# A decoder layer on one core: constants on GpSimd's queue, h's steps behind the eviction, background sums moved between stages

## The chip, the cores and the metric

The kernel runs on 1 core of one Trainium2 chip. The core has TensorE (PE in the profile; PEld is its weight load), VectorE (DVE), ScalarE (ACT), GpSimd (POOL) and SyncE (SP); SP and GpSimd also issue DMAs from queues of their own, and each engine runs its instructions in the order of its own queue. The metric is the device time of one execution in microseconds; lower is better. Three runs of the kernel before took 1571.95, 1572.47 and 1573.18 us, median 1572.47.

## The reference

One layer of a decoder trunk in float32, with 256 tokens (T) and a model width of 2048 (D). Cut to what matters here:

```python
mod = jax.nn.silu(c) @ w_ada[l] + b_ada[l]
shift1, scale1, gate1, shift2, scale2, gate2 = jnp.split(mod[:, None, :], N_MOD, axis=-1)
h = rms_norm(x, norm1_gain[l]) * (1 + scale1) + shift1
x = x + gate1 * mixing_sublayer(h, w_in[l], ...)
h = rms_norm(x, norm2_gain[l]) * (1 + scale2) + shift2
x = x + gate2 * swiglu(h, w_ffn_in[l], w_ffn_out[l])

# mixing_sublayer
proj = h @ w_in
(q_sb, k_sb, v_sb, q_dil, k_dil, v_dil, q_gla, k_gla, v_gla, r_gla, a_gla, gate_cols) = jnp.split(proj, idx, axis=-1)
qb = rms_norm(split_heads(q_dil, DIL_HEADS), dil_q_gain)
kb = rms_norm(split_heads(k_dil, DIL_HEADS), dil_k_gain)
o_dil = merge_heads(dilated_mixture(qb, kb, split_heads(v_dil, DIL_HEADS), alibi_slopes(DIL_HEADS)))
g = jax.nn.sigmoid(gate_cols.reshape(b, t, N_BRANCH, d))
y = g[:, :, 0] * (o_sb @ w_br_sb) + g[:, :, 1] * (o_dil @ w_br_dil) + g[:, :, 2] * (o_gla @ w_br_gla)
return y @ w_out
```

The conditioning vector c gives six rows of 2048 numbers (adaLN): shift, scale and gate for the mixer and for the FFN. The mixer has three branches (stick-breaking attention, dilated windows, gated linear attention, GLA), each behind a sigmoid gate.

## The kernel before

**Products.** Every float32 product is done as three products of a shorter kind: a tile of weights (raw, 128 x 1024, two k-rows of 512 columns, 512 KB) is cast to its high part on ScalarE (whi, L179 or L255), the rest is subtracted on VectorE (wlo, L180 or L241, "the split" below), and TensorE takes high x high (L187), high x low (L188) and low x high (L189). A chunk of weights is two k-rows for two token tiles: twelve matmuls of 512 columns. load_weights issues the loads on SP's queue, ahead of use, into raw buffers that come free when cast and split have read them.

**Stages, by time of the profile.** Up to about 205 us the activations h of the mixer are made chunk by chunk, as the columns of shift1 and scale1 come in, and the blocks of w_in are visited over part of k each (visit: seed a PSUM bank with the partial result, L650; products; evict it, L643). One chunk of h is two steps on ScalarE (make_h: L606 for the high part, L610 for the whole) and a subtraction on VectorE (L611). Then the constants of the attention branches are loaded (L926 to L934: k_low, k_bias, k_lvl, w_gla_a, k_dist). To about 400 the rest of the projection, stick-breaking and GLA run. Then comes the norm of the dilated rows (qk_norm: squares L955 on ScalarE, a chain of small instructions L413 to L421, multiplies L963 on VectorE), while TensorE computes blocks 13 and 14 of w_in; among those are the transposes of the normed rows (qk_turn, L975). From 440 gate blocks are computed, from 486 to 590 three gate pairs by a product with fewer multiplications (gate_pair, fast_products, whose sums and differences are VectorE's L221, L241, L292 and L335 to L338), then the branches' y blocks to 660, gate block 3 with the last y block to about 755, w_out to about 860, and the FFN to the end.

**Background work.** The other four rows of adaLN are computed in the background of these stages. A step (ada_segment_steps) loads half a column block of w_ada, 512 KB (L433, on GpSimd's queue), into a buffer of a ring (tags such as AR0, AR1, OD, KC, KD) and sums an earlier one on VectorE against silu(c) (column_mac, L440, "a sum" below, 1.28 us). The function tick paces them: each chunk of weights adds state["rate"], and a step is done when the total reaches one. So a rate of 0.7 is seven steps in ten chunks. A sum is ordered behind the instruction in state["split"], as a rule the last split. L448 and spread (L370 to L393) turn a finished segment's columns into what its users read.

**What sets the order.** The program text and priorities do, through a scheduler that fills each engine's queue; tc.issue_after(x) keeps an instruction behind x in that order, and prio() raises a load or a cast ahead. A queue is then strict: an instruction that waits holds all behind it on its engine.

The rates of the kernel before are:

```python
RATE_IN, RATE_MID, RATE_GATES, RATE_PAIRS, RATE_Y, RATE_LAST = 0.7, 0.7, 0.65, (0.3, 0.12, 0.12), 0.65, 0.68
RATES_OP, RATES_FFN = (0.4, 0.3, 0.0), (0.75, 0.9, 0.7, 0.6)
RATE_FIRST, RATE_NEXT = 0.95, 0.9
```

Of the kernel before, what the change touches and what calls it, by code (L numbers as in the profile page):

```python
# [13 lines left out]
AF = mybir.ActivationFunctionType  # L14
ALU = mybir.AluOpType
# [15 lines left out]
N_DIL = 6  # L31
N_GLA = 4
SEG_SHIFT1, SEG_SCALE1, SEG_GATE1, SEG_SHIFT2, SEG_SCALE2, SEG_GATE2 = range(6)
RATE_IN, RATE_MID, RATE_GATES, RATE_PAIRS, RATE_Y, RATE_LAST = 0.7, 0.7, 0.65, (0.3, 0.12, 0.12), 0.65, 0.68

RATES_OP, RATES_FFN = (0.4, 0.3, 0.0), (0.75, 0.9, 0.7, 0.6)
LOOK = 3
DEFER = 4
AHEAD = 4000
WARM = (8, 2, 2, 2, 1, 2, 2, 4)  # L40
BADA = 58
RATE_FIRST, RATE_NEXT = 0.95, 0.9
BLOCKS_X, BLOCKS_Y, BLOCKS_Z = (1, 2, 3, 4), (5, 6, 7, 8), (9, 10, 11, 12, 0)
TWO = 3
VISITS = ((BLOCKS_Z, 1, 5, 5, 7), (BLOCKS_Y, 3, 7, 7, 9), (BLOCKS_X, 4, 9, 9, 11),
# [15 lines left out]
RANK = 16  # L61
# [25 lines left out]
def trunk(ctx: ExitStack, tc: tile.TileContext, I, out):  # L87
# [69 lines left out]
    def load_weights(src, k0, k1, b, spare=(), ahead=True, late=None):  # L157

        parts = []
        step, w = 2, NB
        with prio() if ahead else nullcontext():
            for ka in range(k0, k1, step):
                n = min(step, k1 - ka)
                raw = raw_tile(state.get("load_raws", ()))
                state["load"] = nc.sync.dma_start(raw[:, :n, :], src[b, :, ka : ka + n, :])
                i = len(spare) - (k1 - ka)
                if i >= 0:  # L170
                    hi = S(spare[i], [P, step, w], F32R)
                    lo = S(spare[i + 1], [P, step, w], F32R)
                else:
                    hi = wp.tile([P, step, w], F32R, tag="whi", name=nm("whi"), bufs=4)
                    lo = wp.tile([P, step, w], F32R, tag="wlo", name=nm("wlo"), bufs=4)
                if i >= 0 and late is not None:
                    state["casts_after"] = late
                with tc.issue_after(state["casts_after"]) if "casts_after" in state else nullcontext():
                    state["cast"] = nc.scalar.copy(hi[:, :n, :], raw[:, :n, :])  # L179
                state["split"] = nc.vector.tensor_tensor(lo[:, :n, :], raw[:, :n, :], hi[:, :n, :].bitcast(F32), op=ALU.subtract)  # L180
                parts += [(hi[:, i, :], lo[:, i, :]) for i in range(n)]
        if late is not None:
            state.pop("casts_after", None)
        return parts
# [294 lines left out]
            if seg == SEG_SCALE1:  # L479
                scaled_gain(mod1[seg], ROW_N1, k, k + 1)  # L480

    def h_due():
        if "h_due" in state:
            make_h(state.pop("h_due"), after=state["cast"])

    def ada_chunks(k0, k1):

# [111 lines left out]
    def make_h(k, early=False, after=None):  # L599

        sh, sc = gains(k)
        src = xT[k // 4][:, k % 4, :]
        hf = scr([P, T])
        hi = hT[0][k // 4][:, k % 4, :]
        with tc.issue_after(after.ins if hasattr(after, "ins") else after) if after is not None else nullcontext():
            nc.scalar.activation(hi, src, AF.Identity, bias=sh, scale=sc)  # L606
        if early:
            nc.vector.tensor_scalar(hf, src, sc, sh, op0=ALU.mult, op1=ALU.add)
        else:
            nc.scalar.activation(hf, src, AF.Identity, bias=sh, scale=sc)  # L610
        nc.vector.tensor_tensor(hT[1][k // 4][:, k % 4, :], hf, hi.bitcast(F32), op=ALU.subtract)  # L611

    def h_at(k, t):
# [9 lines left out]
    def proj_block(k0, k1, b, w=None, carry=False, steps=None, bank=acc_bank):  # L623
        go_on = bool(carried)
        pss = carried.pop() if go_on else [bank([P, NB]) for _ in range(NT)]
        seeded = A[b] is not None and not go_on
        if seeded:

            with prio():
                for t in range(NT):  # L630
                    nc.scalar.copy(pss[t], A[b][:, t, :])
        block(pss, h_at, w_in, k0, k1, b, w=w, go_on=go_on or seeded, more=carry, seeded=seeded or go_on, steps=steps)
        if carry:
            carried.append(pss)
            return
        evict(b, pss)

    def evict(b, pss):
        with prio():
            if A[b] is None:  # L640
                A[b] = S(f"A{b}", [P, NT, NB])
            for t in range(NT):
                nc.scalar.copy(A[b][:, t, :], pss[t])  # L643

    pending = []

# [5 lines left out]
    def visit(k0, k1, b, bank, carry):  # L652
        pss = [bank([P, NB]) for _ in range(NT)]
        seed(b, pss)
        w = load_weights(w_in, k0, k1, b)
        with tc.issue_after(state["cast"].ins):
            for _ in range(min(2, len(pending))):
                evict(*pending.pop(0))
        h_due()
        block(pss, h_at, w_in, k0, k1, b, w=w, go_on=True, more=carry, seeded=True)  # L660
        (carried if carry else pending).append(pss if carry else (b, pss))

# [260 lines left out]
    lvl_f = S("T4", [P, len(GLA_LEVELS) + 1, P])  # L923
    wga = kc[: 2 * RANK, 4:8, :].rearrange("p a b -> p (a b)")
    with prio():
        nc.sync.dma_start(low, I["k_low"])  # L926
        nc.sync.dma_start(bias, I["k_bias"])
        nc.sync.dma_start(lvl_f, I["k_lvl"])
        for i in range(2):
            nc.sync.dma_start(wga[i * RANK : (i + 1) * RANK, :], I["w_gla_a"])  # L930
    nc.scalar.copy(low_r, low)
    nc.gpsimd.tensor_copy(lvl, lvl_f)
    nc.sync.dma_start(near, I["k_dist"][:, 0:2, :])
    nc.sync.dma_start(far, I["k_dist"][:, 2, :])  # L934

    def head(c, t):
        return A[c // 4][:, t, (c % 4) * P : (c % 4 + 1) * P]
# [7 lines left out]
    def qk_norm(parts):  # L945

        n = sum(h1 - h0 for _, h0, h1, _ in parts)
        ss = small([P, NT, n])
        places, o = [], 0
        for b, h0, h1, _ in parts:  # L950
            for t in range(NT):
                for h in range(h0, h1):
                    junk = scr([P, P])
                    i = o + h - h0
                    nc.scalar.activation(junk, heads(b)[:, t, h, :], AF.Square, accum_out=ss[:, t, i : i + 1])  # L955
            places.append(slice(o, o + h1 - h0))
            o += h1 - h0
        r = rsqrt(ss.rearrange("p t h -> p (t h)"), 1.0 / P, [P, NT * n])
        r = r.rearrange("p (t h) -> p t h", t=NT)
        for (b, h0, h1, _), c in zip(parts, places):  # L960
            for t in range(NT):
                v = heads(b)[:, t, h0:h1, :]
                state["split"] = nc.vector.tensor_tensor(  # L963
                    v, v, r[:, t, c].unsqueeze(2).to_broadcast([P, h1 - h0, P]), op=ALU.mult
                )

# [329 lines left out]
        state[name] = quarters  # L1296

    def background():
        for seg in (SEG_SHIFT2, SEG_SCALE2, SEG_GATE1, SEG_GATE2):
            v = gate2_v if seg == SEG_GATE2 else columns_of(f"mod_{seg}")  # L1300
            done = {SEG_GATE1: lambda: rows_of("gate1", v, ("T4", "T5")), SEG_GATE2: lambda: None}.get(seg, lambda: columns(seg, v))
            yield from ada_segment_steps(v, seg, done())
        yield from last_macs()
# [16 lines left out]
    qk_turn(sb_parts[:2], state["mm"].ins)  # L1320
    sb_hi, sb_lo, sb_step = stick_breaking()
    og, og_norms = gla()
    state["rate"] = RATE_NEXT
    for b in range(6, 9):
        proj_block(*LAST[b], b)
    qk_norm(dil_parts)

# [48 lines left out]
    def sums_of_h(p0, n, scratch, tags):  # L1376
        j, c = p0 // 2, slice(0, 2 * n)
        full = S(scratch[0], [P, 4, T])[:, c]
        with tc.issue_after(state["split"].ins):
            nc.vector.tensor_tensor(full, hT[0][j][:, c].bitcast(F32), hT[1][j][:, c].bitcast(F32), op=ALU.add)  # L1380
        sf = S(scratch[1], [P, 4, 2, P])[:, :, :n]
        sums_of(sf, [full[:, :, t * P : (t + 1) * P] for t in range(NT)], slice(0, 2 * n, 2), slice(1, 2 * n, 2))
        if n == 2:
            hi, lo = (S(tag, [P, 4, n, P], F32R) for tag in tags)
        else:
            hl = S(tags[0], [P, 2, 4, n, P], F32R)
            hi, lo = hl[:, 0], hl[:, 1]
        nc.scalar.copy(hi, sf)
        state["split"] = nc.vector.tensor_tensor(lo, sf, hi.bitcast(F32), op=ALU.subtract)
        for m in range(n):  # L1390
            h_sums[p0 + m] = [(hi[:, i, m, :], lo[:, i, m, :]) for i in range(4)]
# [10 lines left out]
    del state["turns"]  # L1402
    gate_block(0, 1, turns)
    sums_of_h(6, 1, ("X1", "X2"), ("T3",))
    gate_block(0, 2)


# [84 lines left out]
    state["raws"] = -1  # L1492
    gate_pair(0, GATE_PAIRS_2, acc_bank, misc_bank, (("X1", "X2"), ("A9", "A10")), ("T0",))
    gate_pair(1, GATE_PAIRS_3, misc_bank, acc_bank, (("A9", "A10"), ("X1", "T0"), ("T4", "T5")), ("X2", "A8"))
    gate_pair(2, GATE_PAIRS_3, acc_bank, misc_bank, (("A9", "A10"), ("T4", "T5")), ("T0", "X2"))
    ring["tags"] = ("AR0", "AR1", "KC", "KD")
    ring["spare"] = 2
# [335 lines left out]
```

## Time and profile before

| | |
|---|---|
| median of 3 runs | 1572.47 us |
| profiled execution, its own time | 1574.92 us |
| its span | 1573.2 us |
| mean granted clock of TensorE | 0.995 |
| ScalarE busy | 919.4 us (58%) |
| GpSimd busy | 72.1 us (5%) |
| data moved | 399.21 MB, mean 254 GB/s |

A page of the profile lists busy times, waits, groups of instructions and DMAs. In a row of waits stand the engine and line that waited, what it waited for, the total, the number and the longest. In a timeline a row is start, duration, engine, line, operation, output and input tiles, and in brackets the idle time before it with what ended it. In a row of windows stand the stretch, its length, then busy time and instructions of PE, PEld, DVE, ACT and POOL, then the granted clock of TensorE (1.00 is full), the mean busy share of the DMA engines, and GB/s. The span is the time from the first to the last instruction; the execution's own time has a little more around it, 1.7 us here.

### The profile page before, as it was taken

The page shows a single profiled execution, that of the slowest core. Times are in us where ns is not written, and L with a number is a line of the kernel's source. Part 1 is how long each engine was busy: PE and PEld are TensorE (multiplying, and loading weights), DVE is VectorE, ACT ScalarE, POOL GpSimd, SP SyncE. Part 2 cuts the span into 40 slices and gives each one's busy share as a digit, 9 for nine tenths or more (in the row PEclk, how much of TensorE's full clock was granted, in tenths as well). Part 3 has the DMA queues.
Part 4 walks back from the last instruction along what each step waited for, and adds up shares of the span by engine and source line. Part 5 has one row for each costly group of instructions (what it writes and reads, how often), then busy time and mean ns, then how long its engine had stood idle before and what let it go on. Part 6 is the DMA issues. An engine that isn't in the chain of part 4 may idle for free.

```text
span 1573.2 us, 20109 instructions
## 1 busy us (share of the span) xinstructions
PE 1549.8 (99%) x7055; PEld 1279.9 (81%) x7055; DVE 1371.3 (87%) x1838; ACT 919.4 (58%) x1294; POOL 72.1 (5%) x139
## 2 busy tenths in 40 slices
PE   9999999999899999999999999999999999999998
PEld 7788878888687878888888888788888888888887
DVE  7898967888788989987977888999999999789886
ACT  7887776865575555444445645556555555455553
POOL 0000010101100000111100000000000000000000
PEclk9999999999899999999999999999999999999999
DMA  9999897767587767999986686665666567656664
GB/s 371 399 388 352 305 365 272 232 205 235 198 305 244 240 233 227 339 330 329 390 279 214 227 293 206 196 205 194 203 203 203 175 200 247 191 190 196 220 212 136
DMA packets 113749, 399.21 MB, mean 254 GB/s; under 512 B 12496, under 2 KB 13392, under 8 KB 113648
## 3 DMA queue, kind: packets, MB, share of 16 engines
q1 hardware_dynamic: 94640, 328.72, 60.7%
q0 software_dynamic: 19008, 69.21, 13.0%
q8 instruction: 55, 0.90, 0.2%
q14 instruction: 46, 0.38, 0.1%
HBM read 393.69 MB, written 4.19 MB: 253 GB/s over the span
## 4 chain that ended last, share of the span: by engine, by line
PE 74%; DVE 13%; issue 5%; DMA 5%; ACT 3%; POOL 0%; DVEq 0%; ACTq 0%; POOLq 0%; SPq 0%
PE acc L188 17%; PE acc L189 17%; PE acc L187 17%; PE misc L188 6%; PE misc L189 6%; PE misc L187 6%; DVE wlo L241 3%; DMA raw<-w_in 2%; DVE A L241 1%; DMA X<-w_in 1%; DVE T L241 1%; DVE OD L241 1%; DVE KD L241 1%; DMA OS<-ada_t 1%; PE misc L1128 1%
## 5 line engine op out<-in xcount | busy, mean ns | idle before, releaser
L188 PE MATMUL acc<-wlo,H 128*128 128x512 f32 (+1 forms) x856 | 335.4, 392 | 4.2 <-DVE wlo L241 2.8
L187 PE MATMUL acc<-whi,H 128*128 128x512 f32 (+1 forms) x856 | 334.9, 393 | 1.9 <-ACT acc L650 1.1
L189 PE MATMUL acc<-whi,H 128*128 128x512 f32 (+1 forms) x856 | 335.3, 392 | 0.1
L179 ACT CAST whi<-raw 128x1024 fp32r<-128x1024 f32 (+1 forms) x172 | 177.4, 1037 | 149.6 <-PE acc L189 90.9
L180 DVE TENSOR_TENSOR wlo<-raw,whi 128x1024 fp32r<-128x1024 f32 (+1 forms) x172 | 205.4, 1201 | 48.5 <-ACT whi L179 46.9
L188 PEld LDWEIGHTS acc<-wlo,H 128*128 128x128 f32 x856 | 161.6, 189 | 38.8 <-DVE wlo L241 3.8
L187 PEld LDWEIGHTS acc<-whi,H 128*128 128x128 f32 x856 | 161.4, 189 | 35.8 <-ACT acc L650 1.5
L189 PEld LDWEIGHTS acc<-whi,H 128*128 128x128 f32 x856 | 161.5, 189 | 33.6 <-DVE H L1571 0.5
L255 ACT CAST whi<-raw 128x1024 fp32r<-128x1024 f32 (+1 forms) x129 | 124.2, 975 | 75.8 <-PE acc L189 32.1
L241 DVE TENSOR_TENSOR wlo<-raw,whi 128x1024 fp32r<-128x1024 f32 (+1 forms) x129 | 143.3, 1124 | 17.4 <-ACT whi L255 16.1
L189 PE MATMUL misc<-whi,H 128*128 128x512 f32 x285 | 110.5, 388 | 0.0
L188 PE MATMUL misc<-wlo,H 128*128 128x512 f32 x285 | 110.4, 388 | 0.0
L187 PE MATMUL misc<-whi,H 128*128 128x512 f32 x285 | 109.4, 388 | 0.0
L189 PE MATMUL acc<-whi,A 128*128 128x512 f32 x221 | 86.0, 389 | 0.0
L187 PE MATMUL acc<-whi,A 128*128 128x512 f32 x210 | 82.1, 391 | 0.0
L188 PE MATMUL acc<-wlo,A 128*128 128x512 f32 x210 | 81.7, 389 | 0.0
L179 ACT CAST whi<-X 128x1024 fp32r<-128x1024 f32 (+1 forms) x49 | 48.7, 999 | 41.0 <-PE acc L189 31.9
L180 DVE TENSOR_TENSOR wlo<-X,whi 128x1024 fp32r<-128x1024 f32 (+1 forms) x49 | 56.4, 1155 | 15.4 <-ACT whi L179 15.3
L188 PEld LDWEIGHTS misc<-wlo,H 128*128 128x128 f32 x285 | 53.5, 188 | 11.0
L189 PEld LDWEIGHTS misc<-whi,H 128*128 128x128 f32 x285 | 53.5, 188 | 11.0
L187 PEld LDWEIGHTS misc<-whi,H 128*128 128x128 f32 x285 | 53.5, 188 | 10.9
L241 DVE TENSOR_TENSOR A<-raw,A 128x1024 fp32r<-128x1024 f32 (+2 forms) x58 | 55.5, 962 | 2.4 <-ACT A L255 2.0
(753 smaller groups left out, 3376.0 us busy)
## 6 DMA issues: line engine op xcount, KB each, us to landing
raw<-w_ffn_in SPq DMA_DIRECT2D x137, 512.0 KB, 4.6
raw<-w_in SPq DMA_DIRECT2D x129, 512.0 KB, 6.1
raw<-w_ffn_out SPq DMA_DIRECT2D x74, 512.0 KB, 4.3
AR<-ada_t POOLq DMA_DIRECT2D x61, 512.0 KB, 6.9
X<-w_in SPq DMA_DIRECT2D x36, 512.0 KB, 6.2
OS<-ada_t SPq DMA_DIRECT2D x29, 512.0 KB, 7.4
KC<-ada_t POOLq DMA_DIRECT2D x21, 512.0 KB, 7.6
AR<-w_ffn_in SPq DMA_DIRECT2D x21, 512.0 KB, 4.7
```

The source lines that it names most:

```text
L179: state["cast"] = nc.scalar.copy(hi[:, :n, :], raw[:, :n, :])
L180: state["split"] = nc.vector.tensor_tensor(lo[:, :n, :], raw[:, :n, :], hi[:, :n, :].bitcast(F32), op=ALU.subtract)
L187: nc.tensor.matmul(ps, lh, rh, start=start, stop=False, skip_group_check=seeded)
L188: nc.tensor.matmul(ps, lh, rl, start=False, stop=False, skip_group_check=seeded)
L189: state["mm"] = nc.tensor.matmul(ps, ll, rh, start=False, stop=stop, skip_group_check=seeded)
L241: done = nc.vector.tensor_tensor(dst, x, y, op=ALU.subtract)
L255: nc.scalar.copy(hi[:, :n, :], src)
L1128: nc.tensor.matmul(ps[:n, t * N_GLA + h, :].rearrange("p (s l) -> p s l", l=L), at(f, h, t)[:, :n], odd(at(f, h, t)), start=True, stop=True,)
```

## The change

The rates are set anew; RATE_NORM is added. In block 8 of the projection and from gate block (0, 2) on there are fewer steps, in the gate pairs about half or less, and in gate block 3, w_out and the FFN more. The constants are issued by GpSimd instead of SP. In make_h both steps stand behind the instruction given (before, only the first one did), and in visit that is the last copy of an eviction, where there is one. The multiplies of qk_norm are no longer what later sums are ordered behind. The gate row's segment (GATE1) is computed ahead of SCALE2. Ahead of the third gate pair the turn of the raw buffers is set to 1.

```diff
-RATE_IN, RATE_MID, RATE_GATES, RATE_PAIRS, RATE_Y, RATE_LAST = 0.7, 0.7, 0.65, (0.3, 0.12, 0.12), 0.65, 0.68
-RATES_OP, RATES_FFN = (0.4, 0.3, 0.0), (0.75, 0.9, 0.7, 0.6)
+RATE_IN, RATE_MID, RATE_GATES, RATE_PAIRS, RATE_Y, RATE_LAST = 0.7, 0.8, 0.65, (0.15, 0.05, 0.05), 0.7, 0.75
+RATES_OP, RATES_FFN = (0.75, 0.6, 0.0), (0.75, 1.0, 0.9, 0.6)
-RATE_FIRST, RATE_NEXT = 0.95, 0.9
+RATE_FIRST, RATE_NEXT, RATE_NORM = 0.95, 0.9, 0.3
...
-    def h_due():
+    def h_due(after=None):
         if "h_due" in state:
-            make_h(state.pop("h_due"), after=state["cast"])
+            make_h(state.pop("h_due"), after=after or state["cast"])
...
-        with tc.issue_after(after.ins if hasattr(after, "ins") else after) if after is not None else nullcontext():
+        with tc.issue_after(after.ins) if after is not None else nullcontext():
             nc.scalar.activation(hi, src, AF.Identity, bias=sh, scale=sc)
-        if early:
-            nc.vector.tensor_scalar(hf, src, sc, sh, op0=ALU.mult, op1=ALU.add)
-        else:
-            nc.scalar.activation(hf, src, AF.Identity, bias=sh, scale=sc)
+            if early:
+                nc.vector.tensor_scalar(hf, src, sc, sh, op0=ALU.mult, op1=ALU.add)
+            else:
+                nc.scalar.activation(hf, src, AF.Identity, bias=sh, scale=sc)
...
-                nc.scalar.copy(A[b][:, t, :], pss[t])
+                done = nc.scalar.copy(A[b][:, t, :], pss[t])
+        return done
...
+        done = None
         with tc.issue_after(state["cast"].ins):
             for _ in range(min(2, len(pending))):
-                evict(*pending.pop(0))
-        h_due()
+                done = evict(*pending.pop(0))
+        h_due(done)
...
-        nc.sync.dma_start(low, I["k_low"])
-        nc.sync.dma_start(bias, I["k_bias"])
-        nc.sync.dma_start(lvl_f, I["k_lvl"])
+        nc.gpsimd.dma_start(low, I["k_low"])
+        nc.gpsimd.dma_start(bias, I["k_bias"])
+        nc.gpsimd.dma_start(lvl_f, I["k_lvl"])
         for i in range(2):
-            nc.sync.dma_start(wga[i * RANK : (i + 1) * RANK, :], I["w_gla_a"])
+            nc.gpsimd.dma_start(wga[i * RANK : (i + 1) * RANK, :], I["w_gla_a"])
     nc.scalar.copy(low_r, low)
     nc.gpsimd.tensor_copy(lvl, lvl_f)
-    nc.sync.dma_start(near, I["k_dist"][:, 0:2, :])
-    nc.sync.dma_start(far, I["k_dist"][:, 2, :])
+    nc.gpsimd.dma_start(near, I["k_dist"][:, 0:2, :])
+    nc.gpsimd.dma_start(far, I["k_dist"][:, 2, :])
...
-                state["split"] = nc.vector.tensor_tensor(
+                nc.vector.tensor_tensor(
                     v, v, r[:, t, c].unsqueeze(2).to_broadcast([P, h1 - h0, P]), op=ALU.mult
                 )
...
-        for seg in (SEG_SHIFT2, SEG_SCALE2, SEG_GATE1, SEG_GATE2):
+        for seg in (SEG_SHIFT2, SEG_GATE1, SEG_SCALE2, SEG_GATE2):
...
-    state["rate"] = RATE_NEXT
     for b in range(6, 9):
+        state["rate"] = RATE_NEXT if b < 8 else RATE_NORM
         proj_block(*LAST[b], b)
     qk_norm(dil_parts)
...
     sums_of_h(6, 1, ("X1", "X2"), ("T3",))
+    state["rate"] = RATE_NORM
     gate_block(0, 2)
...
+    state["raws"] = 1
     gate_pair(2, GATE_PAIRS_3, acc_bank, misc_bank, (("A9", "A10"), ("T4", "T5")), ("T0", "X2"))
```

The constants on SP's queue, at the end of the visits (OS and AR, X, raw are tiles; w_in rows are weights). Before:

```order
L433 DMA OS_411_1912<-ada_t 128x1024
L433 DMA OS_412_1915<-ada_t 128x1024
L926 DMA T_416_1924<-k_low 128x128
L927 DMA KC_1922<-k_bias 128x128
L928 DMA T_419_1927<-k_lvl 128x1024
L930 DMA KC_1922<-w_gla_a 16x512 x2
L168 DMA raw_1938<-w_in 128x1024
L168 DMA raw_1944<-w_in 128x1024
```

Now:

```order
L433 DMA OS_411_1912<-ada_t 128x1024
L433 DMA OS_412_1915<-ada_t 128x1024
L168 DMA raw_1938<-w_in 128x1024
L168 DMA raw_1944<-w_in 128x1024
L168 DMA raw_1950<-w_in 128x1024
```

The weights follow the column loads without the four rows between. On GpSimd's queue, as a piece of the difference from the program's first loads of background columns (ada_t) on:

```order
+L936 DMA X_418_1926<-k_dist 128x384
+L929 DMA KC_1922<-k_bias 128x128
+L932 DMA KC_1922<-w_gla_a 16x512 x2
+L935 DMA KD_1925<-k_dist 128x768
 L433 DMA OD_1983<-ada_t 128x1024
+L930 DMA T_419_1927<-k_lvl 128x1024
+L928 DMA T_416_1924<-k_low 128x128
+L934 CAST KC_1922<-T_419_1927 128x1024
 L433 DMA AR_445_2027<-ada_t 128x1024
 L433 DMA AR_429_1969<-ada_t 128x1024
-L932 CAST KC_1922<-T_419_1927 128x1024
 L433 DMA AR_446_2042<-ada_t 128x1024
```

The constants stand ahead of the first column loads, and the cast of the levels ahead of the second and third (line numbers are two to four higher in the changed kernel).

VectorE around the norm of the dilated rows, from its first small instruction (L413) on (ISA rows of L440 are the sums, the short one beside each reads its result; L180 rows are splits). Before, to the first multiply:

```order
L413 TENSOR_SCALAR tiny_3409<-tiny_3360 128x24
L440 ISA AR_813_3693,mod_3497<-AR_813_3693,ada_90,mod_3497 128x1024
L440 ISA mod_3497 128x1
L180 TENSOR_TENSOR wlo_3917<-X_850_3914,whi_3916 128x1024
L418 TENSOR_TENSOR tiny_3414<-tiny_3411 128x24
L419 TENSOR_TENSOR tiny_3414<-tiny_3414,tiny_3409 128x24
L420 TENSOR_SCALAR tiny_3414<-tiny_3414 128x24
L180 TENSOR_TENSOR wlo_3923<-X_853_3920,whi_3922 128x1024
L421 TENSOR_TENSOR tiny_3411<-tiny_3411,tiny_3414 128x24
L963 TENSOR_TENSOR A_78_342<-A_78_342,tiny_3411 128x256 x2
```

Now; the next two rows behind these are L421 and the first multiply (L965 here):

```order
L413 TENSOR_SCALAR tiny_3406<-tiny_3357 128x24
L440 ISA AR_810_3648,mod_3521<-AR_810_3648,ada_90,vec 128x1024
L440 ISA mod_3521 128x1
L180 TENSOR_TENSOR wlo_3908<-raw_3905,whi_3907 128x1024
L418 TENSOR_TENSOR tiny_3411<-tiny_3408 128x24
L440 ISA KC_3663,mod_3521<-KC_3663,ada_90,mod_3521 128x1024
L440 ISA mod_3521 128x1
L419 TENSOR_TENSOR tiny_3411<-tiny_3411,tiny_3406 128x24
L440 ISA OD_3690,mod_3521<-OD_3690,ada_90,vec 128x1024
L440 ISA mod_3521 128x1
L180 TENSOR_TENSOR wlo_3914<-X_849_3911,whi_3913 128x1024
L420 TENSOR_SCALAR tiny_3411<-tiny_3411 128x24
```

The chain begins one split earlier in the block of weights, and two sums that stood ahead of L413 or behind the norm now stand within it.

VectorE near the beginning of the first gate pair (L1438, L1441 now, are steps of the mixture of the dilated groups; L1380 and L221 make the sums of h, L1382 now). Before:

```order
L241 TENSOR_TENSOR wlo_4562<-A_982_4548,whi_4561 128x1024
L1438 SCALAR_TENSOR_TENSOR A_958_4485<-misc_4486,vec,A_957_4484 128x2x128
L1438 SCALAR_TENSOR_TENSOR A_958_4485<-misc_4495,vec,A_957_4484 128x2x128
L1380 TENSOR_TENSOR X_961_4504<-H_9_101,H_13_105 128x1024
L241 TENSOR_TENSOR wlo_4600<-raw_4597,whi_4599 128x1024
L221 TENSOR_TENSOR X_962_4506<-X_961_4504 128x256 x2
L221 TENSOR_TENSOR X_962_4506<-X_962_4506,X_961_4504 128x256
L241 TENSOR_TENSOR wlo_4606<-raw_4603,whi_4605 128x1024
L221 TENSOR_TENSOR X_962_4506<-X_961_4504,X_962_4506 128x256
L440 ISA AR_949_4380,mod_3497<-AR_949_4380,ada_90,mod_3497 128x1024
L440 ISA mod_3497 128x1
L440 ISA AR_950_4407,mod_3497<-AR_950_4407,ada_90,vec 128x1024
```

Now:

```order
L1441 SCALAR_TENSOR_TENSOR A_951_4456<-misc_4457,vec,A_950_4455 128x2x128
L1441 SCALAR_TENSOR_TENSOR A_951_4456<-misc_4466,vec,A_950_4455 128x2x128
L1441 SCALAR_TENSOR_TENSOR A_955_4476<-misc_4477,vec,A_954_4475 128x2x128
L1441 SCALAR_TENSOR_TENSOR A_955_4476<-misc_4486,vec,A_954_4475 128x2x128
L1391 TENSOR_TENSOR T_961_4503<-X_959_4497,T_960_4502 128x1024
L241 TENSOR_TENSOR wlo_4553<-A_979_4539,whi_4552 128x1024
L241 TENSOR_TENSOR X_977_4535<-raw_4530,X_976_4534 128x1024
L241 TENSOR_TENSOR wlo_4591<-raw_4588,whi_4590 128x1024
L1441 SCALAR_TENSOR_TENSOR A_955_4476<-misc_4486,vec,A_954_4475 128x2x128
L241 TENSOR_TENSOR wlo_4597<-raw_4594,whi_4596 128x1024
L440 ISA AR_916_4260,mod_3521<-AR_916_4260,ada_90,vec 128x1024
L440 ISA mod_3521 128x1
```

The sums of h stand ahead of these rows now, with the last of them (L1391) and a fast product's parts (A_979, X_977) before the two splits of plain weights (wlo_4591, wlo_4597; wlo_4600 and wlo_4606 before), and one sum instead of two follows.

## The prediction

> **What bounds the kernel now.** I read the page's busy times first, then TensorE's waits, then the granted clock by windows, then the timelines around each long wait.
>
> ```profile
> PE 1549.8 (99%) x7055; PEld 1279.9 (81%) x7055; DVE 1371.3 (87%) x1838; ACT 919.4 (58%) x1294; POOL 72.1 (5%) x139
> PE misc L975 <- DVE A L963: 7.0, 1, 7.0
> PE acc L188 <- DVE wlo L241: 2.8, 2, 1.9
> PE acc L188 <- DVE wlo L180: 1.4, 3, 0.5
> PE acc L187 <- ACT acc L650: 1.1, 1, 1.1
> PE acc L187 <- ACT whi L179: 0.6, 1, 0.6
> 404.78:415.02 10.24, 6.01 (x20) 4.91 (x21) 8.62 (x17) 1.95 (x3) 0.53 (x1) 0.50 0.50 174
> 500.36:503.77 3.41, 3.41 (x10) 2.58 (x9) 3.41 (x7) 1.36 (x2) 0.00 (x0) 0.50 0.70 179
> ```
>
> TensorE is the bound. It stands idle for 1573.2 - 1549.8 = 23.4 us in all, and two windows run at half the granted clock (0.50 in the third column from the right). The change adds and removes no matmul of the products, so it can win only from these waits and the slow windows behind them, and it can lose by making new ones. Five of the waits lie where the diff edits.
>
> **Cost of a wait.** At full clock matmuls of 512 columns start 0.227 us apart:
>
> ```profile
> 497.41 0.39 PE L189 MATMUL acc<-whi,H 128*128 128x512 f32 x1
> 497.64 0.39 PE L187 MATMUL acc<-whi,H 128*128 128x512 f32 x1
> 499.95 0.50 PE L188 MATMUL acc<-wlo,H 128*128 128x512 f32 x1 [1.92 <-DVE wlo L241]
> 409.01 0.69 PE L975 MATMUL misc<-ident,A 128*128 128x128 f32 x2 [7.04 <-DVE A L963]
> ```
>
> 497.64 to 499.95 is 2.31 us, so 2.1 were lost, and 3.41 us of half clock follow, in which 10 matmuls start where 3.41 / 0.227 = 15 would: 5 x 0.227 = 1.1 lost, at most 3.41 / 2 = 1.7; I take 1.4. Together 3.5. The long wait costs 7.2, and of its slow window 415.02 - 409.01 = 6.0 us lie behind it, half of them lost: 3.0, together **10.2**. [...]
>
> **The change part by part.**
>
> 1. *L610 and L606 behind the eviction.*
>
> ```profile
> 64.65 0.60 ACT L610 ACTIVATE scr<-T,shift,scale 128x256 f32<-128x256 f32 x1 [3.14 <-DVE shift L440]
> 65.16 1.04 ACT L179 CAST whi<-AR 128x1024 fp32r<-128x1024 f32 x1
> 67.05 1.12 ACT L650 COPY acc<-A 128x512 f32<-128x512 f32 x2
> 67.70 0.50 PE L187 MATMUL acc<-whi,H 128*128 128x512 f32 x1 [1.12 <-ACT acc L650]
> ```
>
> ScalarE stands 3.14 us before a step of h that waits for VectorE's column, and the cast, the eviction and the seed (L650) that TensorE wants stand behind it. In the new order the step follows them. TensorE lost 1.1 by the row, 1.3 from start to start; the seed can come 3 us earlier, so I take **-1.3** (0 to -1.3: h then comes behind the seed, 68.2 instead of 65.2, and its first use is a later chunk). A like wait of 3.15 us at 184.3 cost 0.5 and goes with the next point.
>
> 2. *Constants by GpSimd.*
>
> ```profile
> SPq L926 <- DVE scale L448: 9.6, 1, 9.6
> 191.63 0.33 SPq L926 DMA_DIRECT2D T<-k_low  x1
> 193.94 1.79 SPq L168 DMA_DIRECT2D raw<-w_in  x4
> 200.07 1.05 ACT L179 CAST whi<-raw 128x1024 fp32r<-128x1024 f32 x1 [1.36 <-DMA raw<-w_in]
> 203.34 1.05 ACT L179 CAST whi<-raw 128x1024 fp32r<-128x1024 f32 x1 [2.23 <-DMA raw<-w_in]
> ```
>
> SP's queue waits 9.6 us to load k_low into a tile that VectorE's last column sums still use, and the weights stand behind it until 193.94. The casts then wait for them, and TensorE for the casts and splits: 1.4 + 0.6 us by its waits, 2.6 from start to start (one of these gaps at 186.4, three from 200.2 to 205.7). Without those rows SP can issue the weights up to 9.6 us sooner, more than enough: **-2.6** (0 to -2.6). GpSimd now holds the waits: behind them in its queue stand the first background columns (AR), which come some 2 to 3 us later, behind the four-row cast of the levels too; their sums stand among the first of the background, where nothing of TensorE's waits on them.
>
> 3. *The norm of the dilated rows.* This is the largest term.
>
> ```profile
> 398.39 0.29 ACT L955 ACTIVATE scr<-A 128x128 f32<-128x128 f32 x1
> 400.48 0.17 DVE L413 TENSOR_SCALAR tiny<-tiny 128x24 f32<-128x24 f32 x1
> 404.31 1.28 DVE L440 CUSTOM_DVE_ANT_0 AR<-AR,ada,mod 128x1024 f32<-128x1024 f32 x1 [3.66 <-DMA AR<-ada_t]
> 405.52 1.22 DVE L180 TENSOR_TENSOR wlo<-X,whi 128x1024 fp32r<-128x1024 f32 x1
> 408.53 1.96 DVE L963 TENSOR_TENSOR A<-A,tiny 128x256 f32<-128x256 f32 x4
> 396.17 0.53 POOL L433 DMA_DIRECT2D AR<-ada_t  x1 [1.81 <-DVE mod L440]
> ```
>
> VectorE reaches a background sum (L440) whose columns were issued only at 396.17 and land 8.1 us later; the norm (L418 to L963) stands behind it. In the new order this sum is another one, loaded earlier, and the squares on ScalarE end about one chunk (2.7 us, twelve matmuls of 0.227) sooner. I laid the new rows out with the durations above, from L413 at about 396: one sum 1.28, one split 1.22, L418, a sum, L419, a sum, a split, L420, L421 and the first multiply, or 3 x 1.28 + 2 x 1.22 + 4 x 0.2 + 0.5 = 7.6, and 0.5 for ScalarE's two steps: the first multiply ends near 404. The transposes stand six matmuls sooner in TensorE's order, so it comes to them at 409.01 - 7.04 - 6 x 0.227 = 400.6. The two sums ahead of L420 have loads issued when the sums before them on the same buffers end, by my layout at 391.9 and 393, so that at 8.1 us they come by 401, just in time. A gap of some 3.5 stays, with one slow window (1.4): 4.9 of 10.2, so **-5** (0 if the last sum's load is late as now, -10 if nothing waits). The end near 404 decides.
>
> 4. *Fewer sums around the gate pairs.*
>
> ```profile
> 486.78 0.69 DVE L241 TENSOR_TENSOR A<-T,raw 128x512 f32<-128x512 f32 x1 [2.61 <-DMA T<-w_in]
> 498.68 1.21 DVE L241 TENSOR_TENSOR wlo<-raw,whi 128x1024 fp32r<-128x1024 f32 x1
> 570.83 0.69 DVE L241 TENSOR_TENSOR A<-raw,raw 128x512 f32<-128x512 f32 x1 [3.27 <-DMA raw<-w_in]
> 577.28 0.49 PE L187 MATMUL acc<-whi,H 128*128 128x512 f32 x1 [0.26 <-ACT whi L255]
> 578.63 0.50 PE L188 MATMUL acc<-wlo,H 128*128 128x512 f32 x1 [0.86 <-DVE wlo L241]
> ```
>
> Counted in the order, 14 sums stand within the three pairs now and 6 after it. Ahead of the first late split (498.68) five sums of 1.28 stand from 475.86 on, then two: 3.8 us less. But the sums of h and other splits are moved ahead of it as well, and the wait of 2.61 for the T tile, which must be read before it is loaded again, stays. I take 1.5 of the 3.5 (0 to 3.5): **-1.5**. In the third pair L187 and L188 lost 0.4 and 1.1; VectorE stood 3.27 us for a buffer of weights, and there the diff adds one buffer (state raws 1) and removes sums: **-1.5** (0 to -1.5).
>
> 5. *The sums put later.* The eight sums go mostly to gate block 3 and w_out; there they cost only if VectorE or the DMAs run out.
>
> ```profile
> 630.00:680.00 50.00, 50.00 (x230) 41.55 (x229) 50.00 (x68) 20.68 (x22) 5.81 (x11) 1.00 0.95 353
> 790.00:860.00 70.00, 70.00 (x309) 57.64 (x307) 51.14 (x62) 32.95 (x44) 5.85 (x11) 1.00 0.72 239
> 703.80 0.53 POOL L433 DMA_DIRECT2D KC<-ada_t  x1 [1.80 <-DVE mod L440]
> 712.66 1.29 DVE L440 CUSTOM_DVE_ANT_0 KC<-KC,ada,mod 128x1024 f32<-128x1024 f32 x1 [4.47 <-DMA KC<-ada_t]
> 715.01 2.35 DVE L180 TENSOR_TENSOR wlo<-raw,whi 128x1024 fp32r<-128x1024 f32 x2
> 715.51 0.39 PE L188 MATMUL acc<-wlo,H 128*128 128x512 f32 x1
> ```
>
> In w_out a chunk takes 2.72 us, and VectorE needs 1.22 + 0.75 x 1.28 = 2.2 of it; the DMAs 512 KB + 0.75 x 512 KB, 338 GB/s, against the 353 of the window from 630. The window from 790 has 19 us of VectorE free, and ten more sums there are 12.8. So it fits, but closely. At 712.66 a sum waited 4.47 for its column and the split behind it ended when the next began, at about 715.1, 0.4 before its use. I put **+1** for a new wait of this kind (0 to +5). The gate row's spreading also moves earlier; on VectorE it is a few instructions of L413's kind (0.17), which I count as nothing.
>
> Sum: -1.3 - 2.6 - 5 - 1.5 - 1.5 + 1 = -10.9. The profiled execution took 1574.92 us, 2.45 over the median 1572.47, so 1564.0 by its own scale and about **1562** (1561.6) by the median's.
>
> **Rivals.**
>
> *All five waits go*: -1.3 - 2.6 - 10.2 - 3.5 - 1.5 = -19.1, about 1553. For it: in the norm only the load of one sum is late, and the squares come sooner. Against: from L413 to L963 the new order still has three sums.
>
> *The norm keeps its wait*: one of the two sums ahead of L420 finds its column late, as now with 8.1 us to land. Then 10.9 falls by the 5, and 1.5 with no help in the first pair: -4.4, about 1568.
>
> *Late columns in gate block 3 and w_out*, which ends slower: with sums at 0.75 per chunk on the same rings, waits like that of 712.66 come through to TensorE. A lead of 4.9 (4.47 + 0.4) covers the present one. A column that comes 5 us later still costs 5 and a slow window, 6.4. Without the +1 the gain is 11.9: two of these (12.8) end at 1573, from where it turns, and three at 1580; I put it at 1576. For it: the DMA share of 0.95 from 630 to 680, with VectorE busy all of 50 us. Against: the one such wait there now is did not reach TensorE, and w_out has 19 us free.
>
> *The constants do not come free*: GpSimd's queue waits, k_low lands late, and the cast of it that stands among the casts of weights at 198 holds ScalarE as SP did. Then point 2 gives nothing and 1564 remains. [...]
>
> ```profile
> AR<-ada_t POOLq DMA_DIRECT2D x61, 512.0 KB, 6.9
> OS<-ada_t SPq DMA_DIRECT2D x29, 512.0 KB, 7.4
> ```
>
> **How the numbers follow.** Forecast (1557 to 1566) 0.55; all waits go 0.15; norm keeps its wait 0.13; late columns 0.11; constants not free 0.06. About 0.2%, 3.1 us, is what a measurement of this kernel can tell from no change, so faster means under 1569.3: the first two, two thirds of the norm's rival (1568 is near the edge) and nearly all of the last, 0.84. Of late columns half end within 0.2% and half above, which with the rest of the others gives same 0.10 and slower 0.06. The range runs from 1553, where all waits go, to 1571, where the unknown costs (norm 0, new wait +5) add up; it leaves out about 0.15.
>
> **What would show it.** Right: no wait of SP's queue near 182 to 191 and no gaps of TensorE at 200 to 206; no wait for L650 at 66; the wait for L963 at 3 to 4 us and a half-clock window of one or two times 3.41 near 402; the wait for L241 in the first pair under 1.9; none in the third. Wrong: a wait for a background column ahead of L963 again, TensorE waits behind L440 after 660, or a wait of ScalarE for the cast of k_low. If the sum is wrong it is by the norm first, whose term alone can move by 5 either way.

## The result, and the profile after

| | before | changed |
|---|---|---|
| median of the runs shown | 1572.83 us (4 runs, 1571.95 to 1574.85) | 1559.74 us (4 runs, 1556.63 to 1562.70) |
| ratio, 95% interval | 1 | 0.9915 [0.9893, 0.9937] |
| a second measurement | 1573.66 us (11 runs) | 1561.11 us (4 runs), 0.9917 [0.9902, 0.9933] |
| profiled execution, its span | 1573.2 us | 1560.9 us |

The change makes the kernel 0.8% faster. The forecast was 1562, with 1553 to 1571. The profiled execution of the changed kernel took 1562.7 us and is the slowest of its four, which matters below. From its page, the busy times; from its waits of TensorE, those in the stages that the change touches (waited for, total, times, longest); from its windows, the stretch behind the norm, whose third column from the right is the granted clock:

```profile
PE 1546.2 (99%) x7055; PEld 1279.0 (82%) x7055; DVE 1371.0 (88%) x1838; ACT 919.2 (59%) x1294; POOL 75.6 (5%) x146
PE misc L977 <- DVE A L965: 2.8, 1, 2.8
PE acc L188 <- DVE wlo L180: 1.4, 1, 1.4
PE misc L188 <- DVE X L241: 0.5, 1, 0.5
399.63:403.04 3.41, 3.41 (x13) 2.72 (x12) 3.40 (x6) 1.63 (x2) 0.00 (x0) 0.50 0.86 347
```

The norm's wait (L975 by L963 before) is down from 7.0 to 2.8, its half-clock window from 10.24 to 3.41. The waits for the seed (L650) and for casts and splits at 200 to 206 are gone; of the first gate pair 0.5 is left, without a slow window. The 1.4 for a split is new. Two of the signs that the prediction named as wrong are there as well, both small: a background sum ahead of L965 that waits for its column (0.88, below), and this late split behind late columns after 660.

Both kernels start 7055 matmuls, so the start of the n-th one in each gives where time went. This table is worked out from the starts in the two traces (changed minus before):

```
stretch of before, us       gained   forecast   what is there
0 to 74                      -1.3      -1.3     seed behind h's step
74 to 214                    -3.1      -2.6     SP's queue at k_low
214 to 390                   -0.2
390 to 420                   -5.6      -5       norm, with its slow window
420 to 484                   +1.1               transposes of the mixture
484 to 509                   -3.6      -1.5     first gate pair
509 to 601                   -1.8      -1.5     third gate pair
601 to 778                   +1.9      +1       gate block 3, start of w_out
778 to the end               +0.4
sum                         -12.2     -10.9
```

VectorE's timeline around the norm (start, duration, line, tiles, idle time and its releaser):

```profile
390.74 0.17 DVE L413 TENSOR_SCALAR tiny<-tiny 128x24 f32<-128x24 f32 x1
390.82 1.28 DVE L440 CUSTOM_DVE_ANT_0 AR<-AR,ada,vec 128x1024 f32<-128x1024 f32 x1
...
393.26 1.28 DVE L440 CUSTOM_DVE_ANT_0 KC<-KC,ada,mod 128x1024 f32<-128x1024 f32 x1
...
395.52 1.29 DVE L440 CUSTOM_DVE_ANT_0 OD<-OD,ada,vec 128x1024 f32<-128x1024 f32 x1 [0.88 <-DMA OD<-ada_t]
...
398.29 0.42 DVE L965 TENSOR_TENSOR A<-A,tiny 128x256 f32<-128x256 f32 x1
```

From L413 to the end of the first multiply (398.71) it takes 8.0 us, laid out as 7.6 + 0.5; on the clock of the kernel before (4.64 us later here) it ends at 403.3, forecast 404. Three sums stand in the chain and the last still waits 0.88 for its column.

Ahead of the split that was late in the first gate pair two sums stand from 460 us on (466.8 and 470.2), where five stood. The wait for the T tile stays, 1.77 us instead of 2.61:

```profile
475.44 0.69 DVE L241 TENSOR_TENSOR A<-T,raw 128x512 f32<-128x512 f32 x1 [1.77 <-DMA T<-w_in]
```

The new wait, in VectorE's timeline of the start of w_out and TensorE's:

```profile
740.76 1.28 DVE L440 CUSTOM_DVE_ANT_0 AR<-AR,ada,vec 128x1024 f32<-128x1024 f32 x1 [1.35 <-DMA AR<-ada_t]
...
745.13 1.28 DVE L440 CUSTOM_DVE_ANT_0 AR<-AR,ada,mod 128x1024 f32<-128x1024 f32 x1 [1.94 <-DMA AR<-ada_t]
...
755.20 2.35 DVE L180 TENSOR_TENSOR wlo<-raw,whi 128x1024 fp32r<-128x1024 f32 x2
...
756.47 0.50 PE L188 MATMUL acc<-wlo,A 128*128 128x512 f32 x1 [1.41 <-DVE wlo L180]
```

Two sums wait for late columns (1.35 + 1.94), VectorE then runs on to 755 with no wait over 0.27 us, and 10 us behind the second wait a split is late. This fits the rival of late columns, at the price of one small wait. It is read from the timeline; no run set the rates of this stage back.

### The profile page after: what moved, and what is told of

The parts are those of the page before. It is cut to its first block, busy times and chain, and to the rows that moved or that the text cites. A ratio compares the mean times of both kernels' runs of the same rounds, so it can differ in the third digit from the quotient of the medians.

```text
span 1560.9 us, 20116 instructions
## 1 busy us (share of the span) xinstructions
PE 1546.2 (99%) x7055; PEld 1279.0 (82%) x7055; DVE 1371.0 (88%) x1838; ACT 919.2 (59%) x1294; POOL 75.6 (5%) x146
## 4 chain that ended last, share of the span: by engine, by line
PE 61%; issue 24%; DVE 8%; DMA 2%; POOL 2%; ACT 2%; SPq 0%; POOLq 0%; DVEq 0%; ACTq 0%
PE acc L189 12%; PE acc L187 12%; PE acc L188 12%; PE misc L189 7%; PE misc L187 7%; PE misc L188 7%; DVE wlo L241 2%; POOL AR L433 1%; DVE OD L241 1%; DVE KD L241 1%; DMA KD<-ada_t 1%; DVE A L241 1%; PE misc L1130 1%; PE acc L718 1%; DMA AR<-ada_t 0%
## 5 line engine op out<-in xcount | busy, mean ns | idle before, releaser
L180 DVE TENSOR_TENSOR wlo<-raw,whi 128x1024 fp32r<-128x1024 f32 (+1 forms) x172 | 204.9, 1201 | 38.5 <-ACT whi L179 38.1
L180 DVE TENSOR_TENSOR wlo<-X,whi 128x1024 fp32r<-128x1024 f32 (+1 forms) x49 | 56.4, 1155 | 14.7 <-ACT whi L179 14.5
```

## The experiments

All start from the changed kernel, and only the edit shown differs. Runs 1 to 10 are one execution each. Times of one execution beside its kernel before (1570 to 1574) say little about 1 us, since one kernel's executions differ by up to 6; so positions in the traces are used. The first 50 us differed by up to 1.9 us between these traces, whatever the edit; positions are counted from the 200th matmul (50 us) on where that matters.

**1. The edit of qk_norm undone: later sums are again ordered behind its multiplies.**

```diff
-                nc.vector.tensor_tensor(
+                state["split"] = nc.vector.tensor_tensor(
                     v, v, r[:, t, c].unsqueeze(2).to_broadcast([P, h1 - h0, P]), op=ALU.mult
                 )
```

> The changed kernel with one edit undone: later sums are again ordered behind the norm's multiplies. Theory: this edit moves nothing (the next split takes over as the instruction to wait behind before any sum asks for it), and the norm came earlier by the lower rate in block 8. Then TensorE's wait for L965 stays at 2.8 us within 0.5 and the time lies with the four runs of the changed kernel, 1556 to 1563. Rival: leaving the norm unordered is what brought it forward; then the wait goes back toward 7 us and the time rises by 4 to 5 us.

1560.89 us. Wait 2.1, gain of the norm's stage 6.2 (5.6 in the changed kernel). The order of every engine is the same, row for row: load_weights of the next block sets state["split"] again before any sum asks for it. This edit of the change does nothing.

**2. The rate in block 8 undone.**

```diff
-        state["rate"] = RATE_NEXT if b < 8 else RATE_NORM
+        state["rate"] = RATE_NEXT
```

> The changed kernel with the old rate of 0.9 in block 8 instead of 0.3. Theory: the squares and the first small instruction again stand one chunk later, behind two sums more, and a sum again waits for its column ahead of the norm: TensorE's wait for the multiplies is 6 to 8 us, a half-clock window of 7 to 10 us follows, and TensorE reaches the stage behind the norm 4 to 6 us later than the changed kernel does. Rival: the earlier loads or the freed SP queue made the difference; then the wait stays near 3 us.

1558.62 us. The theory fell: the wait was 2.3 and no slow window followed; the stage gained 7.4. From VectorE's timeline:

```profile
392.79 1.28 DVE L440 CUSTOM_DVE_ANT_0 AR<-AR,ada,mod 128x1024 f32<-128x1024 f32 x1
...
394.00 0.18 DVE L413 TENSOR_SCALAR tiny<-tiny 128x24 f32<-128x24 f32 x1
395.00 1.28 DVE L440 CUSTOM_DVE_ANT_0 AR<-AR,ada,vec 128x1024 f32<-128x1024 f32 x1 [0.82 <-DMA AR<-ada_t]
```

The squares are indeed later (L413 at 394.0, not 390.7), but the sum behind waits only 0.82: its column was issued at 387.35, when an AR buffer came free one sum earlier in the turn of buffers than in the kernel before.

**3 and 4. The other rate, and both.** RATE_MID back to 0.7 with 0.3 kept in block 8; then also the edit of run 2.

```diff
-RATE_IN, RATE_MID, RATE_GATES, RATE_PAIRS, RATE_Y, RATE_LAST = 0.7, 0.8, 0.65, (0.15, 0.05, 0.05), 0.7, 0.75
+RATE_IN, RATE_MID, RATE_GATES, RATE_PAIRS, RATE_Y, RATE_LAST = 0.7, 0.7, 0.65, (0.15, 0.05, 0.05), 0.7, 0.75
```

> The changed kernel with RATE_MID, the rate behind the norm, back at 0.7 and 0.3 kept in block 8. Theory from the last runs: either of the two rates alone moves the ring of column buffers out of step, so that no sum within the norm's chain has a column loaded only just before; then TensorE's wait for the multiplies is 2 to 3.5 us, as with both. Rival: 0.8 alone does it (with 0.8 and the old 0.9 in block 8 the wait was 2.3); then the wait is 6 to 8 us here.

> The changed kernel with both rates around the norm undone: 0.9 in block 8 and 0.7 behind it; everything else as changed. Theory: VectorE's order around the norm is then again that of the kernel before, the sum behind the first small instruction waits 3 to 4 us for its column, TensorE waits 6 to 8 us for the multiplies with a half-clock window of 7 to 10 us behind, and the time is 3 to 5 us over the changed kernel's. Rival: the earlier start of the stage and the freed SP queue let the column come sooner; then the wait is under 4 us.

1568.39 and 1569.40 us. The one sum that held the chain, with 0.7 alone, then with both old rates:

```profile
397.35 1.28 DVE L440 CUSTOM_DVE_ANT_0 KC<-KC,ada,mod 128x1024 f32<-128x1024 f32 x1 [2.96 <-DMA KC<-ada_t]
...
402.05 1.28 DVE L440 CUSTOM_DVE_ANT_0 AR<-AR,ada,mod 128x1024 f32<-128x1024 f32 x1 [4.49 <-DMA AR<-ada_t]
```

And TensorE's wait for the multiplies, in the same two runs:

```profile
PE misc L977 <- DVE A L965: 4.4, 1, 4.4
...
PE misc L977 <- DVE A L965: 7.3, 1, 7.3
```

With both undone the old stall is back whole (7.3, slow window 10.24, stage gain 0.1), though the constants and h's steps are the new ones. With 0.7 alone it was 4.4 with a slow window of 6.83, gain 2.7: between theory and rival, because there another sum's column comes late. So the norm's gain is the two rates' work, and as the waits in the chain show, they work through which buffer's turn it is when the chain comes. They do not share it evenly: 0.8 behind the norm without 0.3 in block 8 gave the whole gain (run 2), 0.3 in block 8 without 0.8 about half. Run 3 also lost 2.8 of the first pair's 3.6; how is not shown.

**5. The constants on SP again.**

```diff
-        nc.gpsimd.dma_start(low, I["k_low"])
+        nc.sync.dma_start(low, I["k_low"])
...
-    nc.gpsimd.dma_start(far, I["k_dist"][:, 2, :])
+    nc.sync.dma_start(far, I["k_dist"][:, 2, :])
```

> The changed kernel with the constants issued by SP again. Theory: SP's queue stands 8 to 10 us at the load of k_low near 180 to 190, the weights behind it come late, and TensorE's gaps at 196 to 204 return, 2.1 to 2.6 us in all; the rest as in the changed kernel. Rival: the steps of h that were moved made these gaps go; then TensorE is less than 0.5 us later there.

1561.34 us. SP's wait is back, but TensorE is only 0.6 us later at 214. From SP's waits, its timeline, and TensorE's waits to 215 us:

```profile
SPq L928 <- DVE scale L448: 8.3, 1, 8.3
...
188.30 0.33 SPq L928 DMA_DIRECT2D T<-k_low  x1
...
PE acc L188 <- DVE wlo L180: 0.3, 1, 0.3
```

The mechanism was right and the price too high: k_low is now issued at 188.3, 3.3 us sooner than before (191.63), because h's steps brought VectorE's last sums of that stage forward, and the weights behind it come nearly in time.

**6. h's steps as before.**

```diff
-        h_due(done)
+        h_due()
...
-            if early:
-                nc.vector.tensor_scalar(hf, src, sc, sh, op0=ALU.mult, op1=ALU.add)
-            else:
-                nc.scalar.activation(hf, src, AF.Identity, bias=sh, scale=sc)
+        if early:
+            nc.vector.tensor_scalar(hf, src, sc, sh, op0=ALU.mult, op1=ALU.add)
+        else:
+            nc.scalar.activation(hf, src, AF.Identity, bias=sh, scale=sc)
```

> The changed kernel with both steps of h placed as before (the first behind the last cast, the second free). Theory: TensorE waits for the seed near 66 again, 1.3 us, and the gap near 185 of 0.5 us returns: 1.8 us in all by 195 us. Rival: the input stage is bound by the DMAs, so that these waits return but are made up by 210 us and nothing is left.

1567.91 us. Counted from 50 us, TensorE is 1.5 us later by 74 (the wait for the seed, 1.1, is back) and a gap of 0.5 returns at 187; by 195 it is 2.1 later, and still at 214. The theory held, expected 1.8. That gap stayed away in run 5, so it belongs to h's steps. The rest of what this execution lost came later: at the norm it gained 3.8, not 5.6, with a wait of 3.6 and a slow window of 6.83. With run 5: from 50 to 214 us the steps alone gain 3.9, the constants alone 2.4, both 4.6. Each covers part of the other.

**7 and 8. The rates around the gate pairs.** First only the rates within the pairs, then only the lower rate ahead of them, undone.

```diff
-RATE_IN, RATE_MID, RATE_GATES, RATE_PAIRS, RATE_Y, RATE_LAST = 0.7, 0.8, 0.65, (0.15, 0.05, 0.05), 0.7, 0.75
+RATE_IN, RATE_MID, RATE_GATES, RATE_PAIRS, RATE_Y, RATE_LAST = 0.7, 0.8, 0.65, (0.3, 0.12, 0.12), 0.7, 0.75
```

```diff
-    state["rate"] = RATE_NORM
     gate_block(0, 2)
```

> The changed kernel with the old rates 0.3, 0.12, 0.12 within the gate pairs. Theory: the first pair's stall went because fewer sums stand ahead of the pairs, not within them; then TensorE's position at 510 us stays within 0.5 us of the changed kernel's, and at most 1 us comes back by 590. Rival: the sums within the pairs made both stalls; then 3 us return in the first pair and 1.5 in the third.

> The changed kernel without the rate of 0.3 in gate block (0, 2), so with 0.65 there and the new rates within the pairs. Theory: VectorE's order ahead of the first pair is again that of before, with the sums of h and the plain splits last; TensorE waits 1.5 to 2.2 us there, a half-clock window of 3.4 us follows, and 3 to 3.6 us return by 510. Rival: the pairs' own rates did it; then less than 0.7 us returns.

1560.68 and 1560.72 us. TensorE's wait in the first pair, without the lower rate ahead of it:

```profile
PE acc L188 <- DVE wlo L241: 1.9, 1, 1.9
```

That run lost 3.2 of the pair's 3.6 again. The other lost 0.6 of it, and 0.9 more some 20 us later, so 1.5 by 590 where at most 1 was expected. So the lower rate ahead of the pair made nearly all of the gain, not the rates within it. It leaves three sums fewer ahead of the late split (112 of the program's sums stand there, against 115) and lets the sums of h go earlier; which of the two counts more was not tried. The third pair's gain stayed in both.

**9. The turn of the weight buffers undone.**

```diff
-    state["raws"] = 1
     gate_pair(2, GATE_PAIRS_3, acc_bank, misc_bank, (("A9", "A10"), ("T4", "T5")), ("T0", "X2"))
```

> The changed kernel without setting the turn of the weight buffers to 1 ahead of the third gate pair. Theory: this line alone removed the third pair's stall (the old rates within the pairs did not bring it back); then VectorE again waits 2 to 4 us for a buffer there and 1 to 1.7 us return to TensorE by 590. Rival: the fewer sums ahead of the pairs removed it; then less than 0.4 us returns.

1558.14 us. The theory fell: nothing returned in the third pair. Its 1.7 us were gained in every run of this study, whichever one edit was undone, so what made them stays open: an edit that no run undid, or two of which either is enough.

**10. No sum within the norm's chain.** The sums that are traced behind the norm are ordered behind its last multiply.

```diff
-        with tc.issue_after(state["split"].ins):
+        with tc.issue_after(state.get("macs_after", state["split"]).ins):
             column_mac(v, seg, j, half, raw)
...
-                nc.vector.tensor_tensor(
+                state["norm"] = nc.vector.tensor_tensor(
...
     state["rate"] = RATE_MID
+    state["macs_after"] = state["norm"]
...
         rr.append(r)
+    del state["macs_after"]
```

> The changed kernel with the sums that are traced in the two blocks behind the norm ordered behind the norm's last multiply, so that no sum stands between its first small instruction and its multiplies. In the order the transposes also move 24 rows ahead, 5.4 us. Theory: the three sums of 1.28 and the wait of 0.9 for a column within the chain are what holds the multiplies; without them TensorE waits under 2 us there, with no half-clock window, and the stage to 420 us ends 3 to 4 us sooner. Rival: the chain is held by the squares and the small instructions on ScalarE; then, as TensorE comes 5 us sooner, it waits 4 us or more and nothing is gained.

1567.11 us. The norm's wait is gone, not shortened. The same window in the changed kernel and here (length, then busy PE, PEld, DVE, ACT, POOL):

```profile
380.00:420.00 40.00, 37.19 (x176) 30.80 (x175) 33.08 (x68) 28.25 (x92) 4.23 (x8) 0.96 0.68 225
...
380.00:420.00 40.00, 39.94 (x194) 32.87 (x193) 34.28 (x74) 32.53 (x96) 4.22 (x8) 1.00 0.61 200
```

The stage gained 10.1 of the 10.2 that the prediction put there, 4.5 more than the changed kernel (9.6 and 4.2 more if counted to 430 us, from where the matmuls' order is that of before again). But the sums came due behind the norm, ahead of the gate pairs, and there TensorE waited again, with a slow window of 6.83:

```profile
PE acc L188 <- DVE wlo L241: 3.1, 2, 2.1
PE acc L187 <- ACT whi L255: 1.7, 1, 1.7
```

From 484 to 509 it is 4.3 us worse than the kernel before, 7.9 worse than the changed one.

**11 and 12. The changed kernel again, and run 10 with fewer sums** (run 10 with RATE_MID 0.5).

> The changed kernel itself, for its spread and as the measure for the run beside it. Theory: 1557 to 1563 in each execution, ratio to the kernel before 0.990 to 0.994; the norm's wait 2 to 3 us, with a half-clock window behind it in some executions and not in others, which is part of the spread.

> The sums of the two blocks behind the norm ordered behind its multiplies, as in the run before, and RATE_MID at 0.5 instead of 0.8, so that they aren't all made up ahead of the gate pairs (107 sums stand ahead of the first pair instead of 112). Theory: the norm's wait stays away as in the run before (4 us less there than the changed kernel), and the stalls of the first pair (6 us in that run) don't come: 3 to 5 us faster than the changed kernel, 1554 to 1558. Rival: any bunch of sums behind the norm costs at the pairs or in the stages after them what the norm gains; then it lies at 1559 or above.

The changed kernel: 1561.11 us (4 executions), ratio 0.9917 [0.9902, 0.9933], with a wait of 1.8 at the norm, a little less than expected. The other: 1566.67 us (6 executions), 0.9958 [0.9944, 0.9973]; the rival held. At 778 us it was 19.0 us ahead of the kernel before, 3.5 more than the changed kernel's run beside it (15.5). By the end it had lost 10.8 of the 19.0, while the run beside it gained 1.9 more. In the FFN 21 sums are left instead of 17 (16 in the run beside it). The stretch of the FFN's first fast products, here and in the run beside it:

```profile
950.00:1012.00 62.00, 58.56 (x252) 45.66 (x250) 61.53 (x76) 35.35 (x40) 0.00 (x0) 1.00 0.61 195
...
950.00:1012.00 62.00, 62.00 (x279) 51.45 (x278) 60.57 (x74) 36.57 (x42) 0.00 (x0) 1.00 0.61 197
```

VectorE is busy 61.5 of 62 us here and 60.6 in the run beside it, and TensorE stands 3.4 us here and not at all there. VectorE waits for none of the background columns from 815 to 1060. Its last five sums stand at 938 to 945, directly ahead of this stretch, which has no time left to make them up. Counted by the matmuls, this stretch cost 4.1 of the 10.8. Before it 1.5 went to late splits near 825; from 1012 to 1060 3.0 went, with a slow window of 3.41 at 1014; 2.2 went after that. That the five sums cost all of this was not tried. None of the versions tried beats the changed kernel by more than a single execution can show. No run set back the higher rates from gate block 3 on or the order of the segments.

## Why the prediction was right

1. **The bound** was right: TensorE is busy 99% in both, and every gain is a wait or a slow window that went.
2. **h's steps**: -1.3, measured -1.3; undone, 1.5 came back there, and 2.1 by 195 with the gap at 186. The prediction counted that gap, 0.5, with the constants; it is the steps' (runs 5 and 6).
3. **Constants**: -2.6, measured -3.1 from 74 to 214 with the gap at 186, for both edits together. SP's wait is the cause as described, but the two parts were added as if independent; the constants' own share, with h's steps in place, is 0.6.
4. **The norm**: -5, measured -5.6, with the steps as laid out: TensorE at 400.4 on the clock of before (forecast 400.6), first multiply done at 403.3 (404), one slow window, three sums left in the chain. The prediction said that the waiting sum becomes another one with an earlier load. Runs 2 to 4 show that this is so and that the two rates do it. That 5 met 5.6 is in part luck: the second profile of the same kernel gained 8.0 there, without a slow window. Run 10 shows the full price, about 10, which the rival "all five waits go" had put at 10.2.
5. **The first pair** is the term that was mis-sized: "I take 1.5 of the 3.5", measured 3.6. The step that failed is that the sums of h and the T tile's wait would hold the rest; with both there (the T tile's 1.77), TensorE lost only 0.65 us, and no slow window followed, so the 1.4 of the window went as well.
6. **The third pair**: -1.5, measured -1.8, cause open, so that this term came true is luck as far as the runs show. The buffer's turn, named there, is not it alone.
7. **Sums put later**: +1, measured +1.9, of which 1.6 is the gap at 756, as the rival with late columns has it. Run 12 shows the other form of it, which the prediction didn't have: with four or five sums more in the FFN 10.8 us were lost from 778 on, though no background column is late around the FFN's first fast products: VectorE has no time left there (61.5 of 62 us busy).

The prediction had no term for the +1.1 at the transposes of the mixture; in the second profile it was 0.

With the constants on GpSimd TensorE was 0.6 us further at 214 than in run 5, where the weights stood behind k_low in SP's queue and k_low waited 8.3 us. That loads land sooner from one of the two queues than from the other is not shown: in the page of the kernel before, columns of 512 KB took a median of 6.9 us (AR) and 7.6 us (KC) from issue to landing on GpSimd's queue, and 7.4 us (OS) on SP's.

## What to carry to other kernels

Ask of a queue what stands behind a waiting instruction, and of a pacing rate what it does to the turn of the buffers: here a rate changed at one place moved which column was late at another, and the edit in the norm itself moved nothing. Parts that shorten the same wait need not add (3.9 and 2.4 us alone, 4.6 together, runs 5 and 6); undo each with the other in place before giving either a number. Work taken from a full engine must go to a stage that has time left, and the gain at the place it left has to be read at the end of the program.

## What was not expected of the hardware

Behind TensorE's gap at the norm the granted clock fell to half in nine of these twelve executions (0.50 in the changed kernel's row from 399.63 to 403.04), for 3.41, 6.83 or 10.24 us. The gap at the norm (start to start, beyond the pace of 0.227 us) and the half-clock stretch behind it, worked out from the starts and the clock's record in each trace, were:

```
gap us   half clock us   run
7.47        10.24        both old rates
7.20        10.24        before
4.58         6.83        RATE_MID old
3.79         6.83        h's steps old
2.97         3.41        changed
2.48         none        block 8 old
2.43         3.41        pairs old
2.38         none        gate block (0, 2) old
2.30         3.41        norm ordered (the changed kernel's own order)
2.24         3.41        constants on SP
2.10         3.41        buffers' turn old
1.98         none        changed, again
```

Of the seven gaps from 1.98 to 2.48 us, four had a half-clock stretch behind them and three had none, and the length does not part them: 2.48 had none, 2.10 had one; the stage gained 6.0 to 6.3 us with it and 7.4 to 8.0 without. In the window rows 400 to 403 us of run 2 (gap 2.48) and run 1 (gap 2.30) the granted clock, third from the right, is:

```profile
400.00:403.00 3.00, 3.00 (x21) 2.40 (x19) 3.00 (x5) 1.92 (x3) 0.00 (x0) 1.00 0.61 250
...
400.00:403.00 3.00, 3.00 (x11) 2.25 (x10) 2.88 (x6) 1.35 (x2) 0.00 (x0) 0.51 0.98 395
```

What decided between the two was not varied by any run.

Part of the changed kernel's spread of 6 us is this: its two profiles gained 5.6 and 8.0 at the norm, with and without the window. So a forecast for a wait of some 2 us here has to carry both cases, which lay 1.1 to 2.0 us apart in the stage's gain.
